# Strassen's scheme for the two branch projections of a hybrid decoder layer: seven products of token halves for eight, and the merged result through HBM

## Chip, cores and metric

One core of one Trainium2 chip. The metric is the device time of one execution in microseconds. TensorE is called PE here, VectorE DVE, ScalarE ACT, GpSimd POOL, and SP is the engine that issues most transfers.

## The reference

One layer for a prompt of 1024 tokens and 8 single sample tokens, model width 1024, all in float32. From the normed input one wide projection gives the inputs of two branches (retention, sliding-window attention) and two merge gates. What the change touches is the end of the layer:

```
br_r = jnp.einsum('bte,ed->btd', o_r, w_br_ret)
...
br_s = jnp.einsum('bte,ed->btd', o_s, w_br_swa)
merged = jax.nn.sigmoid(mg_r) * br_r + jax.nn.sigmoid(mg_s) * br_s
y = x + jnp.einsum('btd,de->bte', merged, w_out)
```

`o_r` and `o_s` are the branch outputs (tokens x 1024), `w_br_ret`, `w_br_swa` and `w_out` are 1024 x 1024.

## The kernel before

All matrices are held with the feature on the 128 partitions: 1024 features are 8 blocks (`KT`), the 1032 token columns (`TOK`, prompt and sample together) lie along the free axis. For precision each float32 operand is split into a hi and a lo part of type float32r, and each product is made of three matmuls: hi x hi, hi x lo, lo x hi (`gemm_T`, lines 212 to 214). Weights arrive by `load_unit`: a transfer of 512 KB into `wraw` (three buffers, `RAW`), a hi copy on ACT (line 168), a lo copy on POOL (line 169), with six slots for the pairs (`wbufs`). `run_steps` walks a list of steps and loads weight units a few steps ahead while slots are free.

The order of the work inside an engine is not the order of the program: a planner (the tile framework's scheduler, driven by its own timeline) takes for each engine the earliest instruction in program order that is ready and has a buffer, and the queues then run in that fixed order. A tile pool has a number of buffers per tag, and pools stacked on the left or the right side of SBUF reuse each other's place, tile by tile, when the older pool is closed.

Phase 1 makes the branch outputs. Per group of heads a gated output block is written to HBM (`d_o[0..7]` for retention, `d_o[8..15]` for attention, line 290), and 48 merge-gate blocks (`mg_block`, lines 292 to 299) write tanh values to `d_t`. The last of these merge-gate blocks end phase 1 on PE. Under them `open_a` (line 829) already loads seven of the eight retention operands back through the `oT` tiles (two buffers) and splits them with `split_op` (ACT line 870, DVE line 871) into the pool `opA1`.

`phase23` (line 879) then runs
- retention's projection: for each of 8 output blocks `c` and 3 token thirds `nb` (`BL` = 344 columns) 24 matmuls into one PSUM bank, then `br_r` multiplies with the gate (`tt`, loaded from `d_t`) and writes `d_m`. The eighth operand `opA7` and all eight attention operands `opB0..7` are loaded and split meanwhile, through `st` (two buffers);
- attention's projection in the same loops; `br_s` gates, adds the retention part (`mm`, loaded from `d_m`) and splits the merged block into `mhi` and `mlo`, which stay in SBUF;
- the output projection: two halves of 512 columns, each 8 token tiles and one of sample rows (`out_tile`, lines 943 to 959), with the merged blocks as stationary operand.

All loads and stores of these stages but the `d_t` writes stand in SP's queue.

Of the kernel before, what the change touches and what calls it, by code (L numbers as in the profile page):

```python
# [9 lines left out]
F32 = mybir.dt.float32  # L10
F32R = mybir.dt.float32r
AF = mybir.ActivationFunctionType
ALU = mybir.AluOpType
# [4 lines left out]
P = 128  # L18
# [92 lines left out]
def br_unit(w, c):  # L111
    return ("T", ((w, c * P, P),), 0, KT)


def out_unit(half, j):
    return ("o", (("w_out", half * 512, 512),), 2 * j, 2)
# [6 lines left out]
class Body:  # L123
# [27 lines left out]
    def load_unit(self, spec):  # L151
        nc = self.nc
        kind, segs, k0, nk = spec
# [16 lines left out]
        return view(hi), view(lo)  # L170

# [34 lines left out]
    def gemm_T(self, ps, unit, op, n0):  # L206
        nc = self.nc
        whi, wlo = unit
        cs = slice(n0, n0 + BL)
        for k in range(KT):  # L210
            hi, lo = op[k]
            nc.tensor.matmul(ps, whi[:, k, :], hi[:, cs], start=(k == 0), stop=False)  # L212
            nc.tensor.matmul(ps, whi[:, k, :], lo[:, cs], start=False, stop=False)  # L213
            nc.tensor.matmul(ps, wlo[:, k, :], hi[:, cs], start=False, stop=(k == KT - 1))  # L214

# [432 lines left out]
    def build(self):  # L648
# [4 lines left out]
        with tc.tile_pool(name="const", bufs=1, reuse_waits="tile") as cp, tc.tile_pool(name="sm", bufs=2, reuse_waits="tile") as sm, \  # L653
# [8 lines left out]
            self.d_m = [self.t(dp, [P, TOK], f"d_m{k}") for k in range(8)]  # L662
# [24 lines left out]
    def groups(self):  # L687
# [141 lines left out]
        def open_a(us):  # L829
            use(None)  # L830
            self.pA1 = self.tc.tile_pool(name="opA1", bufs=1, side="right", reuse_waits="tile")
            pool = self.pA1.__enter__()
            self.opA = []
            for k in range(0, NA1, 2):
                st = self.t(self.gp, [P, 2, TOK], "oT", bufs=2)
                for i in range(min(2, NA1 - k)):
                    nc.sync.dma_start(out=st[:, i, :], in_=self.d_o[k + i])
                    self.opA.append(self.split_op(pool, f"opA{k + i}", st[:, i, :], k + i))
        steps.append(([], open_a))
        steps += prev + mg  # L840
        steps.append(([br_unit("w_br_ret", 0), br_unit("w_br_ret", 1)], nop))
# [23 lines left out]
    def split_op(self, pool, tag, src, kt):  # L865
        nc = self.nc
        hi = self.t(pool, [P, TOK], tag + "h", F32R)
        lo = self.t(pool, [P, TOK], tag + "l", F32R)
        sc = self.scales[kt]
        nc.scalar.activation(out=hi[:], in_=src, func=AF.Copy, scale=sc)  # L870
        nc.vector.scalar_tensor_tensor(out=lo[:], in0=src, scalar=sc, in1=hi[:].bitcast(F32), op0=ALU.mult, op1=ALU.subtract)
        return hi, lo

    def load_op(self, pool, tag, kt):
        st = self.t(self.stg, [P, TOK], "st", bufs=2)
        self.nc.sync.dma_start(out=st[:], in_=self.d_o[kt])
        return self.split_op(pool, tag, st[:], kt)

    def phase23(self):
        nc, tc = self.nc, self.tc  # L880
        with tc.tile_pool(name="stg", bufs=1, reuse_waits="tile") as self.stg, tc.tile_pool(name="pacc2", bufs=8, space=PSUM, reuse_waits="tile") as self.pacc:
            pBc = tc.tile_pool(name="opB", bufs=1, reuse_waits="tile")
            pB = pBc.__enter__()
            with tc.tile_pool(name="opA2", bufs=1, side="right", reuse_waits="tile") as pA2:
                opA = self.opA + [self.load_op(pA2, f"opA{k}", k) for k in range(NA1, KT)]
                opB = [self.load_op(pB, f"opB{k}", 8 + k) for k in range(KT)]
                steps = []
                for c in range(KT):
                    for nb in range(NB):
                        steps.append(([br_unit("w_br_ret", c)], lambda us, c=c, nb=nb: self.br_r(us[0], c, nb, opA)))  # L890
                steps.append(([br_unit("w_br_swa", 0), br_unit("w_br_swa", 1)], nop))
                self.run_steps(steps, 2)
            self.pA1.__exit__(None, None, None)
            with tc.tile_pool(name="mrg", bufs=1, side="right", reuse_waits="tile") as pM:
                self.mhi = self.t(pM, [P, KT, TOK], "mhi", F32R)
                self.mlo = self.t(pM, [P, KT, TOK], "mlo", F32R)
                self.ms = self.t(self.stg, [P, KT, MROW], "st", F32R, bufs=2)
                nc.vector.memset(self.ms[:].bitcast(F32), 0.0)
                steps = []
                for c in range(KT):  # L900
                    for nb in range(NB):
                        steps.append(([br_unit("w_br_swa", c)], lambda us, c=c, nb=nb: self.br_s(us[0], c, nb, opB)))
                steps.append((([out_unit(0, j) for j in range(4)]), nop))
                self.run_steps(steps, 2)
                pBc.__exit__(None, None, None)
                steps = []
                with tc.tile_pool(name="fin", bufs=1, reuse_waits="tile") as self.fin:
                    for half in range(2):
                        us = [out_unit(half, j) for j in range(4)]
                        order = list(range(NT + 1)) if half == 0 else [NT] + list(range(NT))  # L910
                        for t in order:
                            steps.append((us, lambda u, half=half, t=t: self.out_tile(u, half, t)))
                    self.run_steps(steps, 4)

    def br_r(self, unit, c, nb, op):
        nc = self.nc
        n0 = nb * BL
        ps = self.t(self.pacc, [P, 512], "acc2")
        self.gemm_T(ps[:, :BL], unit, op, n0)
        tt = self.t(self.stg, [P, BL], "tt", bufs=2)  # L920
        nc.sync.dma_start(out=tt[:], in_=self.d_t[c][:, n0 : n0 + BL])
        nc.vector.scalar_tensor_tensor(out=tt[:], in0=tt[:], scalar=1.0, in1=ps[:, :BL], op0=ALU.add, op1=ALU.mult)
        nc.sync.dma_start(out=self.d_m[c][:, n0 : n0 + BL], in_=tt[:])

    def br_s(self, unit, c, nb, op):
        nc = self.nc
        n0 = nb * BL
        cs = slice(n0, n0 + BL)
        ps = self.t(self.pacc, [P, 512], "acc2")
        self.gemm_T(ps[:, :BL], unit, op, n0)  # L930
        tt = self.t(self.stg, [P, BL], "tt", bufs=2)
        mm = self.t(self.stg, [P, BL], "mm", bufs=2)
        nc.sync.dma_start(out=tt[:], in_=self.d_t[8 + c][:, cs])
        nc.sync.dma_start(out=mm[:], in_=self.d_m[c][:, cs])
        nc.vector.scalar_tensor_tensor(out=tt[:], in0=tt[:], scalar=1.0, in1=ps[:, :BL], op0=ALU.add, op1=ALU.mult)
        nc.vector.tensor_tensor(out=tt[:], in0=tt[:], in1=mm[:], op=ALU.add)
        nc.scalar.activation(out=self.mhi[:, c, cs], in_=tt[:], func=AF.Copy, scale=0.5)
# [49 lines left out]
```

## Time and profile before

| | |
|---|---|
| median of 3 runs (lowest, highest) | 1212.75 us (1212.04, 1216.18) |
| profiled execution, time | 1212.75 us |
| profiled execution, span of its instructions | 1211.0 us |
| mean granted clock of PE | 0.994 |
| PE busy | 1181.9 us (98%) |
| PE weight loads busy | 1115.3 us (92%) |
| DVE, ACT, POOL busy | 668.4, 457.1, 354.8 us |
| first matmul of a branch operand | 928.98 us |

The span is read as four parts: phase 1 up to 929 us, retention's projection up to about 1020, attention's up to about 1111, and the output projection to the end. Busy time of PE counts a matmul from start to modelled end, and matmuls overlap; what one costs in a full stream is the distance between two starts.

### The profile page before, as it was taken

Reading aid. Unit: us, or ns where it says so; the run is one execution under the profiler, and the core shown is the slowest. Engines: PE = TensorE matmul, PEld = TensorE weight load, DVE = VectorE, ACT = ScalarE, POOL = GpSimd, SP = SyncE. Lnnn points to the kernel's source line nnn. Section 1 sums busy time; section 2 is a strip of 40 time slices with the busy share of each in tenths; the row PEclk is TensorE's granted clock in tenths of the full one; section 3 lists DMA queues with packets and bytes.
Section 4 is the critical chain, followed back from the end, with each engine's and each line's share of the span. In section 5 each row is a group of like instructions: output and inputs, shape, how many; then the busy total and the mean of one; then the engine's idle time right before and its main releaser. Section 6 shows DMA issues by size and latency. Waiting matters only on the chain.

```text
span 1211.0 us, 19495 instructions
## 1 busy us (share of the span) xinstructions
PE 1181.9 (98%) x7228; PEld 1115.3 (92%) x7228; DVE 668.4 (55%) x2018; ACT 457.1 (38%) x1158; POOL 354.8 (29%) x282
## 2 busy tenths in 40 slices
PE   5799999999999999999999999999999999999998
PEld 4799999999989999999999999999899999999877
DVE  5455445544544387777776767677853411555121
ACT  5444334344334235554454445444544310221010
POOL 4424216315315433422242224112532122212010
PEclk9899999999999999999999999999999999999999
DMA  8414113223123411210141013101517844554221
GB/s 302 139 48 136 59 42 103 73 68 92 49 66 86 144 51 56 87 53 7 61 128 36 7 48 117 61 7 36 171 48 244 240 146 138 172 158 137 80 88 70
DMA packets 125169, 116.71 MB, mean 96 GB/s; under 512 B 17481, under 2 KB 113225, under 8 KB 125041
## 3 DMA queue, kind: packets, MB, share of 16 engines
q1 hardware_dynamic: 118160, 106.99, 28.5%
q10 hardware_dynamic: 6912, 8.46, 2.0%
q8 instruction: 57, 0.93, 0.3%
q14 instruction: 40, 0.32, 0.1%
HBM read 85.05 MB, written 32.44 MB: 97 GB/s over the span
## 4 chain that ended last, share of the span: by engine, by line
PE 92%; DVE 3%; DMA 1%; ACT 1%; issue 1%; SPq 1%; POOL 0%; ACTq 0%; POOLq 0%
PE acc L212 16%; PE acc L213 16%; PE acc L214 16%; PE acc L224 9%; PE acc L223 9%; PE acc L222 9%; PE tr L546 2%; PE acc L233 1%; PE acc L232 1%; PE av L441 1%; DMA oT<-in_x_prompt 1%; PE sc L532 1%; PE sc L533 1%; PE av L557 1%; DVE s L491 1%; PE av L556 1%
## 5 line engine op out<-in xcount | busy, mean ns | idle before, releaser
L169 POOL TENSOR_TENSOR wlo<-wraw,whi 128x1024 fp32r<-128x1024 f32 (+1 forms) x92 | 205.2, 2237 | 342.6 <-ACT whi L168 277.5
L212 PE MATMUL acc<-hhi,whi 128*128 128x344 f32 x864 | 281.9, 326 | 6.5 <-ACT whi L168 5.9
L213 PE MATMUL acc<-hlo,whi 128*128 128x344 f32 x864 | 279.8, 324 | 0.0
L214 PE MATMUL acc<-hhi,wlo 128*128 128x344 f32 x864 | 278.9, 323 | 0.0
L222 PE MATMUL acc<-whi,hhi 128*128 128x384 f32 x512 | 175.4, 343 | 2.4 <-ACT hhi L139 1.2
L223 PE MATMUL acc<-wlo,hhi 128*128 128x384 f32 x512 | 175.2, 342 | 0.6 <-POOL wlo L169 0.6
L224 PE MATMUL acc<-whi,hlo 128*128 128x384 f32 x512 | 175.3, 342 | 0.0
L212 PEld LDWEIGHTS acc<-hhi,whi 128*128 128x128 f32 x864 | 163.3, 189 | 8.6 <-ACT whi L168 6.2
L213 PEld LDWEIGHTS acc<-hlo,whi 128*128 128x128 f32 x864 | 163.2, 189 | 1.8 <-issue 1.0
L214 PEld LDWEIGHTS acc<-hhi,wlo 128*128 128x128 f32 x864 | 163.1, 189 | 1.4 <-issue 0.6
L147 POOL TENSOR_TENSOR rs<-ms,nhalf 128x1 f32<-128x1 f32 (+3 forms) x81 | 68.4, 846 | 295.1 <-DVE ms L146 286.4
L168 ACT ACTIVATE whi<-wraw 128x1024 fp32r<-128x1024 f32 (+1 forms) x92 | 90.2, 982 | 169.3 <-PE acc L213 106.3
L222 PEld LDWEIGHTS acc<-whi,hhi 128*128 128x128 f32 x512 | 97.5, 191 | 4.0 <-ACT hhi L139 1.6
L223 PEld LDWEIGHTS acc<-wlo,hhi 128*128 128x128 f32 x512 | 97.3, 190 | 2.5 <-POOL wlo L169 1.0
L224 PEld LDWEIGHTS acc<-whi,hlo 128*128 128x128 f32 x512 | 97.2, 190 | 0.5 <-DVE hlo L140 0.2
L486 ACT ACTIVATE s<-s,ng 128x256 f32<-128x256 f32 (+1 forms) x128 | 61.7, 485 | 25.8 <-DVE ng L483 25.7
L288 POOL TENSOR_TENSOR oT<-oT,tg 128x344 f32<-128x344 f32 x48 | 45.7, 954 | 84.9 <-DVE tg L286 62.2
L536 DVE CUSTOM_DVE_ANT_0 s<-sc,band,rs 128x256 f32<-128x256 f32 (+1 forms) x128 | 53.6, 460 | 19.4 <-PE sc L533 19.2
L139 ACT ACTIVATE pThi<-tr 128x512 fp32r<-128x512 f32 x60 | 35.3, 596 | 53.5 <-PE tr L546 53.1
L140 DVE TENSOR_TENSOR pTlo<-tr,pThi 128x512 fp32r<-128x512 f32 x60 | 41.0, 686 | 21.9 <-ACT pThi L139 21.7
L491 DVE TENSOR_SCALAR s<-s,r 128x256 f32<-128x256 f32 (+1 forms) x128 | 52.1, 468 | 0.7
L224 PE MATMUL acc<-whi,mlo 128*128 128x512 f32 x128 | 50.5, 395 | 0.0
(346 smaller groups left out, 2359.5 us busy)
## 6 DMA issues: line engine op xcount, KB each, us to landing
wraw<-in_w_in SPq DMA_DIRECT2D x36, 512.0 KB
d_t<-tg ACTq DMA_DIRECT2D x48, 172.0 KB
d_o<-oT SPq DMA_DIRECT2D x16, 516.0 KB
tt<-d_t SPq DMA_DIRECT2D x48, 172.0 KB
wraw<-in_w_in SPq DMA_DIRECT2D x32, 256.0 KB
st<-d_o SPq DMA_DIRECT2D x9, 516.0 KB
d_m<-tt SPq DMA_DIRECT2D x24, 172.0 KB
mm<-d_m SPq DMA_DIRECT2D x24, 172.0 KB
```

The source lines that it names most:

```text
L147: nc.gpsimd.tensor_tensor(out=rs[:p, :width], in0=ms[:p, :width], in1=self.nhalf[:p, :width], op=ALU.pow)
L168: nc.scalar.activation(out=hi[:, :f], in_=raw[:, :f], func=AF.Copy)
L169: nc.gpsimd.tensor_tensor(out=lo[:, :f], in0=raw[:, :f], in1=hi[:, :f].bitcast(F32), op=ALU.subtract)
L212: nc.tensor.matmul(ps, whi[:, k, :], hi[:, cs], start=(k == 0), stop=False)
L213: nc.tensor.matmul(ps, whi[:, k, :], lo[:, cs], start=False, stop=False)
L214: nc.tensor.matmul(ps, wlo[:, k, :], hi[:, cs], start=False, stop=(k == KT - 1))
L222: nc.tensor.matmul(ps, hi[:, k, a:b], whi[:, kk, :], start=(k == 0), stop=False)
L223: nc.tensor.matmul(ps, hi[:, k, a:b], wlo[:, kk, :], start=False, stop=False)
L224: nc.tensor.matmul(ps, lo[:, k, a:b], whi[:, kk, :], start=False, stop=(k == KT - 1))
L486: nc.scalar.activation(out=s[:p, j, :nk], in_=s[:p, j, :nk], func=AF.Exp, bias=ng[:p, j : j + 1], accum_out=l[:p, j : j + 1])
L491: nc.vector.tensor_scalar(out=s[:p, j, :nk], in0=s[:p, j, :nk], scalar1=r[:p, j : j + 1], scalar2=None, op0=ALU.mult)
L536: nc.vector.tensor_tensor_reduce(out=s[:, j, :nk], in0=sc[:, a, :nk], in1=band, scale=rs[:, j : j + 1], scalar=-3e38, op0=ALU.add, op1=ALU ...
```

## The change

Both branch projections use one level of Strassen's scheme in the form with seven products and shared sums. The two "rows" are two neighbouring output blocks `c` and `c + 1`, the two "columns" of the second operand are the two halves of the tokens, and the inner dimension is cut in two halves of four k-blocks (`j` and `j + 4`). The tokens are also cut in two quarters-of-halves `q` (`QTOK`: 256 columns each for q = 0, 260 for q = 1, which takes the sample tokens too), so that one product has 256 or 260 columns.

- Weights: per pair four parts (`load_part`): block 1, two sums, the changed block 2, one more sum, made by four DVE operations on `wsum` (one buffer) and split like before; 3.5 copies of 1024 columns per pair where there were two.
- Operands: `make_op` loads for one `j` four blocks of a quarter into `raw` (for retention it scales them on ACT), forms four differences on POOL, and splits seven matrices at once, hi on ACT and lo on DVE. A set is four such builds. The set for retention's q = 0 is made in `open_a` through the two `oT` buffers; the other three sets go through `raw` in pool `stg`, which has one buffer. Retention's two sets lie in `opA0` (right) and `opA1` (left); attention's sets take the same places when retention's last pair has used them (`swap`), and the merged blocks take them after that.
- `pair_steps`: seven products of 12 matmuls each, on four PSUM tiles, with three copies out of PSUM on ACT (`keep`) and four sums on DVE (`put`); then the gate as before.
- The merged block is written to HBM (`d_y`) by `br_s` and loaded and split again by `load_merged`, in two quarters; the output tiles of the first half run in the order 0, 1, 4, 5, 2, 3, 6, 7, sample rows.

```diff
+    def load_part(self, w, c, part):
...
+        one, two = self.praw
+        if part == 1:
+            sums = self.sums = self.t(self.sp, [P, 3, 512], "wsum", bufs=1)
+            a11, a12, a21, a22 = one[:, 0:512], one[:, 512:1024], two[:, 0:512], two[:, 512:1024]
+            nc.vector.tensor_tensor(out=sums[:, 1], in0=a21, in1=a22, op=ALU.add)
+            nc.vector.tensor_tensor(out=sums[:, 0], in0=sums[:, 1], in1=a11, op=ALU.subtract)
+            nc.vector.tensor_tensor(out=sums[:, 2], in0=a12, in1=sums[:, 0], op=ALU.subtract)
+            nc.vector.tensor_tensor(out=a21, in0=a11, in1=a21, op=ALU.subtract)
...
+        nc.scalar.activation(out=hi[:, :f], in_=src, func=AF.Copy)
+        nc.gpsimd.tensor_tensor(out=lo[:, :f], in0=src, in1=hi[:, :f].bitcast(F32), op=ALU.subtract)
...
+    def product(self, ps, part, half, op, b, start=True, stop=True):
...
+        for j in range(4):
+            ws = slice(half * 512 + j * P, half * 512 + (j + 1) * P)
+            hi, lo = op[j]
...
+            nc.tensor.matmul(ps[:, :n], whi[:, ws], hi[:, b, :], start=(start and j == 0), stop=False, **kw)
+            nc.tensor.matmul(ps[:, :n], whi[:, ws], lo[:, b, :], start=False, stop=False, **kw)
+            nc.tensor.matmul(ps[:, :n], wlo[:, ws], hi[:, b, :], start=False, stop=(stop and j == 3), **kw)
...
+        def keep():
+            sn = self.t(self.stg, [P, 260], "sn", bufs=3)
+            nc.scalar.activation(out=sn[:, :n], in_=v["X"][:, :n], func=AF.Copy)
+            return sn[:, :n]
...
+        a, m, b, d = units
+        return [([a], p1), ([a], p2), ([m], p6), ([m], p5), ([b], p7), ([b], p4), ([d], p3)]
...
+            raw = lambda: self.t(self.gp, [P, 2, TOK], "oT", bufs=2)[:].rearrange("p a b -> p (a b)")
+            self.opA0 = [self.make_op(pool, raw(), 0, j, 0) for j in range(4)]
...
+    def make_op(self, pool, raw, base, j, q):
+        nc = self.nc
+        n = QTOK[q]
+        r = raw[:, : 8 * n].rearrange("p (a n) -> p a n", a=8)
+        for e in range(2):
+            k = j + 4 * e
+            self.get_quarter(r[:, 2 * e : 2 * e + 2], self.d_o[base + k], q)
+            if base == 0:
+                nc.scalar.activation(out=r[:, 2 * e : 2 * e + 2], in_=r[:, 2 * e : 2 * e + 2], func=AF.Copy, scale=self.scales[k])
+        b12, b11, b22, b21, t1, t2, t3, t4 = [r[:, a] for a in range(8)]
+        for o, a, b in ((t1, b12, b11), (t2, b22, t1), (t3, b22, b12), (t4, t2, b21)):
+            nc.gpsimd.tensor_tensor(out=o, in0=a, in1=b, op=ALU.subtract)
+        hi = self.t(pool, [P, 7, n], f"op{j}h", F32R)
+        lo = self.t(pool, [P, 7, n], f"op{j}l", F32R)
+        nc.scalar.activation(out=hi[:], in_=r[:, 1:], func=AF.Copy)
+        nc.vector.tensor_tensor(out=lo[:], in0=r[:, 1:], in1=hi[:].bitcast(F32), op=ALU.subtract)
...
+        raw = lambda: self.t(self.stg, [P, 8 * 260], "raw", bufs=1)[:]
...
+            ops(("r", 1), 0, 1)(self.pL.__enter__())
+            steps = []
+            for b, w, fin in (("r", "w_br_ret", self.br_r), ("s", "w_br_swa", self.br_s)):
+                for c in range(0, KT, 2):
+                    for q in range(2):
+                        steps += self.pair_steps(w, c, q, (lambda b=b, q=q: op[b, q]), fin)
+                        if c == KT - 2:
+                            attr, side = ("pR", right) if q == 0 else ("pL", left)
+                            if b == "r":
+                                steps.append(swap(attr, lambda side=side, q=q: side(f"opB{q}"), ops(("s", q), 8, q)))
+                            else:
+                                steps.append(swap(attr, lambda side=side, q=q: side(f"m{q}"), merged(q)))
...
+    def load_merged(self, k, q):
...
+        st = self.t(self.stg, [P, 2, 260], "st", bufs=2)
+        hi, lo = self.mq[q]
+        nc.sync.dma_start(out=st[:, :, :n], in_=self.d_y[k, q][:])
+        nc.scalar.activation(out=hi[:, k], in_=st[:, :, :n], func=AF.Copy, scale=0.5)
+        nc.vector.scalar_tensor_tensor(out=lo[:, k], in0=st[:, :, :n], scalar=0.5, in1=hi[:, k].bitcast(F32), op0=ALU.mult, op1=ALU.subtract)
```

## Rows read from the trace of the kernel before

**Rows 1.** The page: busy time by engine, and the last chain by engine.

```profile
PE 1181.9 (98%) x7228; PEld 1115.3 (92%) x7228; DVE 668.4 (55%) x2018; ACT 457.1 (38%) x1158; POOL 354.8 (29%) x282
PE 92%; DVE 3%; DMA 1%; ACT 1%; issue 1%; SPq 1%; POOL 0%; ACTq 0%; POOLq 0%
```

**Rows 2.** Stretches: from:to, length, busy time (instructions) by engine, clock, DMA share, GB/s.

```profile
929.00:1032.00 103.00, 103.00 (x654) 102.81 (x654) 25.98 (x35) 20.30 (x20) 21.72 (x9) 1.00 0.57 174
1032.00:1111.00 79.00, 79.00 (x502) 79.00 (x501) 46.32 (x83) 18.48 (x31) 16.79 (x7) 1.00 0.54 167
1111.00:1211.00 100.00, 96.25 (x416) 75.36 (x415) 18.50 (x25) 4.67 (x6) 7.17 (x3) 1.00 0.23 79
```

**Rows 3.** Timeline of PE: start us, us, instruction; eight of 256 columns, then the next.

```profile
442.76 0.28 PE L532 MATMUL sc<-kThi,qs 128*128 128x256 f32 x1
...
443.71 0.34 PE L224 MATMUL acc<-whi,hlo 128*128 128x384 f32 x1
```

**Rows 4.** Timelines of SP, ACT, DVE: two loads and their first users, [idle before <-releaser].

```profile
946.89 0.32 SPq L876 DMA_DIRECT2D st<-d_o  x1
951.89 1.07 ACT L870 ACTIVATE opB3h<-st 128x1032 fp32r<-128x1032 f32 x1 [3.39 <-DMA st<-d_o]
...
1005.02 0.32 SPq L921 DMA_DIRECT2D tt<-d_t  x1
1007.34 0.51 DVE L922 SCALAR_TENSOR_TENSOR tt<-tt,acc 128x344 f32<-128x344 f32 x1 [4.82 <-DMA tt<-d_t]
```

**Rows 5.** POOL by line and shape: xcount | busy us, mean ns | idle before <-releasers.

```profile
L169 POOL TENSOR_TENSOR wlo<-wraw,whi 128x1024 fp32r<-128x1024 f32 x60 | 144.2, 2407 | 302.7 <-ACT whi L168 246.3 <-PE acc L233 42.8 <-ACT vv L139 5.5
...
L641 POOL TENSOR_TENSOR Aswa_q_g<-s,gbs 128x288 f32<-128x288 f32 x1 | 0.8, 793 | 0.0
```

**Rows 6.** ACT by line and shape.

```profile
L168 ACT ACTIVATE whi<-wraw 128x1024 fp32r<-128x1024 f32 x60 | 63.3, 1057 | 154.4 <-PE acc L213 100.0 <-PE acc L232 43.6 <-DMA wraw<-in_w_in 6.5
...
L139 ACT ACTIVATE pThi<-tr 128x512 fp32r<-128x512 f32 x60 | 35.3, 596 | 53.5 <-PE tr L546 53.1
L168 ACT ACTIVATE whi<-wraw 128x768 fp32r<-128x768 f32 x32 | 26.9, 842 | 14.8 <-PE acc L213 6.3 <-DMA wraw<-in_w_in 4.7 <-PE acc L224 2.0
```

**Rows 7.** Timeline of DVE: lo copies of 1032 columns, the first while POOL works.

```profile
913.25 1.91 DVE L871 SCALAR_TENSOR_TENSOR opA0l<-oT,rng,opA0h 128x1032 fp32r<-128x1032 f32 x1 [0.20 <-ACT opA0h L870]
...
922.19 1.29 DVE L871 SCALAR_TENSOR_TENSOR opA2l<-oT,rng,opA2h 128x1032 fp32r<-128x1032 f32 x1 [5.16 <-ACT opA2h L870]
...
941.45 1.23 DVE L871 SCALAR_TENSOR_TENSOR opB0l<-st,opB0h 128x1032 fp32r<-128x1032 f32 x1 [0.44 <-ACT opB0h L870]
```

**Rows 8.** Timelines of SP and DVE: the first loads of mm and their first use.

```profile
948.81 0.42 SPq L934 DMA_DIRECT2D mm<-d_m  x1
...
1033.78 0.52 DVE L936 TENSOR_TENSOR tt<-tt,mm 128x344 f32<-128x344 f32 x1
```

**Rows 9.** Timeline of PE where the branch projections begin.

```profile
928.98 0.32 PE L212 MATMUL acc<-opA0h,whi 128*128 128x344 f32 x1
...
931.81 0.32 PE L212 MATMUL acc<-opA0h,whi 128*128 128x344 f32 x1
...
939.74 0.75 PE L212 MATMUL acc<-opA7h,whi 128*128 128x344 f32 x3
```

**Rows 10.** Timelines of ACT and SP while open_a loads operands.

```profile
912.07 1.14 ACT L870 ACTIVATE opA0h<-oT,rng 128x1032 fp32r<-128x1032 f32 x1
...
917.06 2.59 SPq L837 DMA_DIRECT2D oT<-d_o  x4
```

**Rows 11.** Stretches around two slow stretches of the clock (columns as in rows 2).

```profile
31.30:38.10 6.80, 4.55 (x14) 4.56 (x15) 1.67 (x4) 3.67 (x6) 4.23 (x3) 0.50 1.04 330
...
857.00:860.70 3.70, 1.90 (x13) 1.48 (x11) 3.70 (x3) 0.46 (x1) 3.40 (x2) 1.00 0.91 245
860.70:864.10 3.40, 3.40 (x13) 3.24 (x14) 3.32 (x14) 1.87 (x4) 0.20 (x1) 0.51 1.03 335
864.10:868.00 3.90, 3.90 (x28) 3.84 (x27) 3.36 (x6) 2.08 (x4) 3.34 (x2) 0.99 0.76 224
```

More of the change, by code (lines that the diff above doesn't have):

```diff
@@ L108, in shape_constants, with pair_units @@
     return {k: np.ascontiguousarray(v.astype(np.float32)) for k, v in out.items()}
-def br_unit(w, c):
-    return ("T", ((w, c * P, P),), 0, KT)
+def pair_units(w, c):
+    return [("S", w, c, part) for part in range(4)]
+HALF = SEQ // 2
+QTOK = (256, 260)
+B11, B22, B21, T1, T2, T3, T4 = range(7)
 def out_unit(half, j):
@@ L152, in load_unit @@
         nc = self.nc
+        if spec[0] == "S":
+            return self.load_part(*spec[1:])
         kind, segs, k0, nk = spec
@@ L830, in open_a @@
             use(None)
[L831 to L838, printed above, removed]
+            self.pS = self.tc.tile_pool(name="wsum", bufs=1, side="right", reuse_waits="tile")
+            self.sp = self.pS.__enter__()
+            self.pR = self.tc.tile_pool(name="opA0", bufs=1, side="right", reuse_waits="tile")
+            pool = self.pR.__enter__()
+            raw = lambda: self.t(self.gp, [P, 2, TOK], "oT", bufs=2)[:].rearrange("p a b -> p (a b)")
+            self.opA0 = [self.make_op(pool, raw(), 0, j, 0) for j in range(4)]
         steps.append(([], open_a))
         steps += prev + mg
-        steps.append(([br_unit("w_br_ret", 0), br_unit("w_br_ret", 1)], nop))
+        steps.append((pair_units("w_br_ret", 0)[:2], nop))
         self.run_steps(steps, 2)
@@ L863, in swa_consts, with quarter, get_quarter @@
             nc.sync.dma_start(out=dst[:], in_=self.i[name][0].rearrange("b k g d -> k b (g d)"))
-    def split_op(self, pool, tag, src, kt):
+    def quarter(self, t, q):
+        return t[:, :SEQ].rearrange("p (h q n) -> p q h n", h=2, q=2)[:, q], t[:, SEQ:].rearrange("p (h n) -> p h n", h=2)
+    def get_quarter(self, dst, src, q):
         nc = self.nc
[L867 to L871, printed above, removed]
+        body, rows = self.quarter(src, q)
+        nc.sync.dma_start(out=dst[:, :, :256], in_=body)
+        if q:
+            nc.sync.dma_start(out=dst[:, :, 256:260], in_=rows)
@@ L872, in split_op @@
         return hi, lo
[L874 to L877, printed above, removed]
     def phase23(self):
         nc, tc = self.nc, self.tc
-        with tc.tile_pool(name="stg", bufs=1, reuse_waits="tile") as self.stg, tc.tile_pool(name="pacc2", bufs=8, space=PSUM, reuse_waits="tile") as self.pacc:
[L882 to L913, printed above, removed]
@@ new lines, in phase23, with swap, fn @@
+        op = {("r", 0): self.opA0}
+        raw = lambda: self.t(self.stg, [P, 8 * 260], "raw", bufs=1)[:]
+        left = lambda name: tc.tile_pool(name=name, bufs=1, reuse_waits="tile")
+        right = lambda name: tc.tile_pool(name=name, bufs=1, side="right", reuse_waits="tile")
+        def swap(attr, mk, fill):
+            def fn(us):
+                getattr(self, attr).__exit__(None, None, None)
+                ctx = mk()
+                setattr(self, attr, ctx)
+                fill(ctx.__enter__())
+            return ([], fn)
@@ new lines, in ops, with fill, merged @@
+        def ops(key, base, q):
+            def fill(pool):
+                op[key] = [self.make_op(pool, raw(), base, j, q) for j in range(4)]
+            return fill
+        def merged(q):
+            def fill(pool):
+                self.mq[q] = tuple(self.t(pool, [P, KT, 2, QTOK[q]], f"m{q}{x}", F32R) for x in "hl")
+                if q:
+                    nc.vector.memset(self.ms[:].bitcast(F32), 0.0)
+                for k in range(KT):
+                    self.load_merged(k, q)
+            return fill
@@ new lines, in phase23 @@
+        with tc.tile_pool(name="stg", bufs=1, reuse_waits="tile") as self.stg, tc.tile_pool(name="pacc2", bufs=8, space=PSUM, reuse_waits="tile") as self.pacc:
+            self.ms = self.t(self.stg, [P, KT, MROW], "ms", F32R)
+            self.mq = {}
+            self.pL = left("opA1")
+            ops(("r", 1), 0, 1)(self.pL.__enter__())
[10 more added lines that the diff above has]
+                                steps.append(swap(attr, lambda side=side, q=q: side(f"m{q}"), merged(q)))
+            for half in range(2):
+                us = [out_unit(half, j) for j in range(4)]
+                order = [0, 1, 4, 5, 2, 3, 6, 7, NT] if half == 0 else [NT] + list(range(NT))
+                for t in order:
+                    steps.append((us, lambda u, half=half, t=t: self.out_tile(u, half, t)))
+            self.run_steps(steps, 4)
+            self.pL.__exit__(None, None, None)
+            self.pR.__exit__(None, None, None)
+            self.pS.__exit__(None, None, None)
```

109 lines of the change are left out of this document (81 added, 28 removed).

## The prediction

> **What bounds the kernel now.** First the engines' table and the chain that ended last [rows 1]: TensorE (PE) is busy for 98% of the span and carries 92% of the chain, so work taken from PE is worth its full price, and anything that makes PE wait costs its full price too. Then the stages the change touches [rows 2]: from 929 to 1032 us PE runs one matmul every 103.0/654 = 157.5 ns and has no idle time, the same from 1032 to 1111; the output projection fills the last 100 us. The branch projections are 2 branches x 8 output blocks x 3 token thirds x 24 = 1152 matmuls of 344 columns, 1152 x 157.5 ns = 181.4 us. Nobody else is near a limit there: from 929 to 1032 VectorE is busy 26 us, ScalarE 20, GpSimd 22 of 103. So the question is only whether PE gets shorter work and stays fed.
>
> **Matmuls: a gain of 20.6 us.** Per pair of output blocks and token quarter there are 7 products x 4 k-pairs x 3 = 84 matmuls; 4 pairs x 2 quarters x 2 branches give 1344, half of 256 columns and half of 260. Eight matmuls of 256 columns back to back start from 442.76 to 443.71, 0.95/8 = 118.8 ns each, every one with its own weight load [rows 3]. Against 157.5 at 344 that is 0.44 ns a column, so 260 columns take 120.5. The mean is 119.6: 1344 x 0.1196 = 160.8 us, 20.6 less. One quarter of one pair (84) is 10.0 us. The bounds: if long trains keep the old pitch of 157.5 the term is +30 us; I see no reason for under 118.
>
> **One operand build: 10.7 to 12.3 us, one after another.** The new operands (7 matrices, hi and lo) are built per k-pair `j`, four builds to a set, in four sets: (ret, q0), (ret, q1), (swa, q0), (swa, q1). Each build is a row of dependent steps: load into `raw`, (ret only) two scalings, four subtractions, one hi copy, one lo copy. Outside the first set `raw` is a tag with one buffer, so the next load waits until the lo copy has read it: nothing overlaps inside a set.
> - Load: two transfers of 256 KB (q1: two small ones more). A load of 172 KB was used 2.3 us after its issue (1005.02 to 1007.34), one of 516 KB 5.0 us after (946.89 to 951.89) [rows 4]. The bytes are those of the second, but that one shared a busy queue; I take the middle, 3.65, and 4.45 for q1, whose two further issues take SP some 0.4 each (0.32 for the instruction [rows 4]). Bounds 2.3 and 5.0.
> - Subtractions on GpSimd, 256 elements: 0.79 us at 288 and 2.41 at 1024 [rows 5], so 2.2 ns an element and 0.72 each, 2.9 for four.
> - Hi copy on ScalarE, 1792 elements: 1.057 at 1024 and 0.842 at 768 [rows 6] give 1.70. The scalings are 0.6 each (0.59 at 512); the first lies beside the second load, so 0.8 counts.
> - Lo copy on VectorE, 1792 elements: 1.23 to 1.29 at 1032 [rows 7], against 0.51 at 344 [rows 4], so 2.05 alone; a first bound of 1.9 and, beside GpSimd, 1.91/1.29 as long, 3.0.
> - Hand-overs: some 0.1 each, 0.4.
>
> Sum: 10.7 (swa, q0), 11.5 (swa, q1), 12.3 (ret, q1); with the bounds together 9.3 to 14.
> The lo copy beside GpSimd took 1.91, without it 1.29 [rows 7]. The Trainium skill, "SBUF — State Buffer", section "Who interferes with whom", says that a VectorE instruction with two SBUF inputs and a GpSimd one that reads SBUF exclude each other for the whole instruction; the trace agrees, and by the rule a lo copy that meets a weight copy would stand up to 2.4 us late, up to 9.6 us a set, where my sum has nothing: four sets late by that would give 1332 instead of 1294.
>
> **What covers a set.** Operands are overwritten in place: a swa set may write its hi and lo only when the ret operands of that quarter have been read for the last time. The planner orders by readiness, not by program order, and fills PE with what it can: before, while the eighth operand was late, PE started three blocks with the seven it had (block two starts at 931.81, before the first is ended, three opA7h in one go at 939.74) [rows 9]. It also loads ahead into a free buffer: `mm` issued at 948.81 is used at 1033.78 [rows 8]. So I grant: (a) the first `raw` of a set is loaded and subtracted ahead where it is free; (b) products of the waiting quarter run for the k-pairs that are there, 4 accumulators x 9 = 36 matmuls, 4.3 us; (c) while a q1 set is awaited, the next pair's q0 runs, but only its first two weight parts fit (six slots, four held by the current pair), 48 matmuls, 5.7 us. More the weight slots do not allow.
> - (swa, q0): its operands are free when ret's last q0 ends. First build 1.70 + 2.05 = 3.8, three more 32.1: 35.9. Cover: ret's last q1, 10.0, and 4.3. **Stall 21.6** (bounds 17 to 30).
> - (swa, q1): `raw` is free only when (swa, q0) is done: 4 x 11.5 = 46. Cover: the other 48 matmuls of q0, 5.7, plus 5.7, plus 4.3 = 15.7. **Stall 30.3** (22 to 38).
> - (ret, q1): `raw` now lies where the two `oT` tiles were, which hold the loads of (ret, q0); so it too starts when that set ends. 4 x 12.3 = 49.2 - 15.7: **stall 33.5** (25 to 46, with weight copies of 2.41 in the same GpSimd queue).
> - (ret, q0): two buffers here, under the merge-gate blocks that end at 928.98 [rows 9]. The first build takes the place of opA0h at 912.07; the loads that need released `oT` come at 917.06 and later [rows 10]. From 917 two builds in a row on one buffer, 11.5 each, end at 940, 11 after PE is free, less 4.3: **stall 7** (3 to 12).
>
> **The rest.** Merged blocks now go to HBM and back (`load_merged`, 8 a quarter, two buffers): 3.3 us for two (load 2.3 and ACT and DVE copies of 512), some 15 us for eight against 10.0 of the last swa q1 and output tiles that start on k-blocks present: 2 (0 to 8). The second quarter's reload lies beside four output tiles of 24 x 0.231 us (96.25/416 in the last stage [rows 2]), 22 us in all, at nothing; without that cover 15. SP's queue holds all loads in planner order; the weight loads for the pairs stand between them and are early by a pair. The sums of weight blocks (four of 512 on VectorE) and 28 instead of 16 weight copies' worth on GpSimd (28 x 2.41 = 67 us of 160) lie beside PE at nothing once it streams. Evictions (`keep`, `put`: under the 0.51 of 344 columns [rows 4]) have one product, 1.4 us, of cover each.
>
> **The clock.** When PE had been idle for half of 857.0 to 860.7, the granted clock stood at 0.51 for the next 3.4 us, 13 matmuls where the next stretch has 28 in 3.9; earlier it stood at 0.50 for 6.8 us [rows 11]: each return costs 1.7 to 3.4 us. Four long stalls: 8 (6.8 to 13.6). The Trainium skill, "TensorE: Matmul & The Clock Gate", Part 1, says that the slow clock is the default and activity lifts it; the trace agrees, and the rule speaks against a change that cuts PE's stream; without it the sum would come to 1286.
>
> **The sum**: -20.6 + 7 + 33.5 + 21.6 + 30.3 + 2 + 8 = +81.8 us. The profiled execution took 1212.75 with a span of 1211.0; it is the median of the runs shown, so nothing is to be added: 1212.75 + 81.8, **1294 us**. With all low ends 1266, with all high ends about 1339.
>
> **Rivals.**
> - *Builds overlap* (the other side). If the steps of a set ran side by side, a build every 2.9 us (GpSimd, the longest), a set would take 3.8 + 8.7 = 12.5, under 14.3 of cover; stalls go to 3, the clock's part to 2, and the time is 1212.75 - 20.6 + 3 + 2 + 2 = 1199. It decides at a set under about 14 us. For it: in the first set, on two buffers, it partly holds. Against it: one `raw` buffer. 0.07.
> - *The planner covers more*: half of the three large stalls go because `raw` finds free memory or more products move ahead: 1294 - 43 = 1251. For it: [rows 9]. Against: six weight slots. 0.13.
> - *The trains do not hold 119 ns*: PE's weight loads are 188 ns long and fill the 344-column stage (102.81 of 103 us [rows 2]). If loads set the pace in long trains, pitch 157.5: 1294 + 51 = 1345. Against: rows 3 have a load each. 0.05.
> - *Queues in planner order run wrong on the chip*: VectorE or ScalarE holds a copy of a build behind an eviction that waits for PE; one eviction's product train (10 us) in each of three sets: 1324. 0.08.
> - That the products are not fewer is excluded by the count, 1344 shorter matmuls.
>
> **How the numbers follow.** Forecast 0.67, rivals as given. The range reaches from the second rival's upper half to the forecast's high end: 1243 to 1338. Faster by over 0.3% (about what a measurement of this kernel can tell from no change) has the first rival and little else, 0.08; within 0.3% 0.02; slower 0.90.
>
> **What would show it.** In the profile after: PE idle four times, for some 7, 33, 22 and 30 us, each ended by the hi or lo tile of the fourth build (`op3h`, `op3l`); `raw` loads one by one, 10 us or more apart; matmuls of 256 columns 119 ns apart in between; the granted clock at half after each stall. Wrong it is if PE stays over 95% busy between 929 us and the end, if raw loads of one set overlap, or if the pitch at 256 columns is over 125 ns.

## The result, and the profile after

| | before | after |
|---|---|---|
| median (lowest, highest) | 1213.45 us (1212.04, 1216.18) | 1318.14 us (1317.50, 1322.59) |
| profiled execution, span | 1211.0 us | 1315.7 us |
| mean granted clock of PE | 0.994 | 0.953 |

The change made the kernel slower: ratio 1.0865, 95% interval 1.0841 to 1.0889, 104.7 us between the medians. The forecast was 1294 us, in a range of 1243 to 1338.

The page of the kernel after, engines and granted clock in 40 slices (before: [rows 1]):

```profile
PE 1194.8 (91%) x7420; PEld 1117.1 (85%) x7420; DVE 748.2 (57%) x2082; ACT 505.0 (38%) x1230; POOL 438.2 (33%) x362
...
PEclk9899999999999999999999999999868967699999
```

PE's share fell from 98% to 91%, and the granted clock dips in the slices of the branch projections. The busy time of PE even rose, from 1181.9 to 1194.8, although its matmuls in the changed stages are cheaper: a matmul at half clock counts for longer. The chain that ended last is of no use here: its shares add up to about a tenth of the span.

The stages of the kernel after, cut at the first matmul of a branch product, at the first use of the fourth operand (`op3l`) of each of the four operand sets, and where retention's last q = 0 product and the stream before the output projection end (columns as in [rows 2], which has the same stages of before):

```profile
core 0: us, PE busy (x) PEld busy (x) DVE busy (x) ACT busy (x) POOL busy (x), PEclk, DMA share, GB/s
927.94:945.27 17.33, 7.61 (x41) 6.71 (x41) 7.51 (x4) 7.61 (x7) 9.97 (x10) 0.82 0.29 89
945.27:991.44 46.17, 22.80 (x120) 20.69 (x120) 11.44 (x11) 13.63 (x15) 11.96 (x16) 0.65 0.43 115
991.44:1057.35 65.91, 62.10 (x488) 60.87 (x489) 35.88 (x46) 19.38 (x35) 31.70 (x18) 0.96 0.49 143
1057.35:1095.11 37.76, 13.99 (x67) 12.11 (x65) 16.69 (x16) 8.76 (x7) 14.32 (x15) 0.60 0.38 114
1095.11:1140.19 45.08, 21.49 (x120) 19.39 (x120) 12.91 (x12) 7.92 (x7) 11.74 (x16) 0.65 0.35 95
1140.19:1207.42 67.23, 62.68 (x501) 61.50 (x501) 43.49 (x53) 20.42 (x36) 32.66 (x14) 0.97 0.57 176
1207.42:1315.70 108.28, 100.99 (x430) 77.60 (x428) 35.50 (x64) 14.61 (x21) 10.12 (x5) 0.98 0.42 136
```

Rows 1, 2, 4 and 5 of the seven are the waits for the four sets, each with few matmuls in a long time; rows 3 and 6 are the streams behind them. Who ended PE's waits, from the first branch product to the output projection (us in total, times, longest):

```profile
PE acc L257 <- ACT op3h L989: 22.0, 4, 7.1
PE acc L257 <- ACT op2h L989: 20.6, 3, 7.8
PE acc L257 <- ACT op1h L989: 15.4, 4, 4.7
PE acc L257 <- ACT sn L273: 7.4, 9, 1.4
PE acc L258 <- DVE op0l L990: 6.1, 1, 6.1
...
PE acc L257 <- DVE cc L280: 3.1, 4, 1.7
```

78 of some 89 us of waiting are for the hi and lo tiles of operand builds. One build, the last of retention's q = 1 set, in the timelines of SP, ACT, POOL and DVE (start, length, what):

```profile
980.13 0.36 SPq L971 DMA_DIRECT2D raw<-d_o  x1
...
991.42 0.87 SPq L971 DMA_DIRECT2D raw<-d_o  x2
...
983.05 0.73 ACT L983 ACTIVATE raw<-raw,rng 128x520 f32<-128x520 f32 x1 [5.04 <-DMA raw<-d_o]
...
987.58 1.72 ACT L989 ACTIVATE op3h<-raw 128x1820 fp32r<-128x1820 f32 x1 [2.27 <-POOL raw L986]
...
985.44 2.11 POOL L986 TENSOR_TENSOR raw<-raw 128x260 f32<-128x260 f32 x3 [0.85 <-ACT raw L983]
...
989.33 2.06 DVE L990 TENSOR_TENSOR op3l<-raw,op3h 128x1820 fp32r<-128x1820 f32 x1 [9.23 <-ACT op3h L989]
```

Load from 980.13, first scaling at 983.05, subtractions to 987.55, hi copy to 989.30, lo copy to 991.39, and only at 991.42 the next load, since `raw` has one buffer: 11.3 us, step behind step, where 12.3 were forecast for this set.

### The profile page after: what moved, and what is told of

It reads as the page before. It is cut to its first block, busy times and chain, and to the rows that moved or that the text cites. A ratio compares the mean times of both kernels' runs of the same rounds, so it can differ in the third digit from the quotient of the medians.

```text
span 1315.7 us, 20230 instructions
## 1 busy us (share of the span) xinstructions
PE 1194.8 (91%) x7420; PEld 1117.1 (85%) x7420; DVE 748.2 (57%) x2082; ACT 505.0 (38%) x1230; POOL 438.2 (33%) x362
## 5 line engine op out<-in xcount | busy, mean ns | idle before, releaser
L176 POOL TENSOR_TENSOR wlo<-wraw,whi 128x1024 fp32r<-128x1024 f32 (+1 forms) x76 | 167.4, 2212 | 187.3 <-ACT whi L175 125.2
L175 ACT ACTIVATE whi<-wraw 128x1024 fp32r<-128x1024 f32 (+1 forms) x76 | 73.3, 967 | 80.4 <-PE acc L246 41.9
L986 POOL TENSOR_TENSOR raw<-raw 128x260 f32<-128x260 f32 (+1 forms) x48 | 35.4, 758 | 91.7 <-DMA raw<-d_o 57.1
L257 PE MATMUL acc<-op3h,whi 128*128 128x260 f32 (+1 forms) x112 | 32.4, 311 | 22.0 <-ACT op3h L989 22.0
```

Source lines behind the costliest of these rows:

```text
L175: nc.scalar.activation(out=hi[:, :f], in_=raw[:, :f], func=AF.Copy)
L176: nc.gpsimd.tensor_tensor(out=lo[:, :f], in0=raw[:, :f], in1=hi[:, :f].bitcast(F32), op=ALU.subtract)
```

## Experiments

Each is an edit of the kernel after. Medians, with the ratio to the kernel before:

| | us | ratio (95%) |
|---|---|---|
| attention uses retention's sets | 1256.75 | 1.0350 (1.0332 to 1.0369) |
| eleven builds reduced to their copies | 1242.32 | 1.0243 (1.0222 to 1.0263) |
| both | 1230.52 | 1.0123 (1.0106 to 1.0140) |
| two `raw`, small buffers cut | 1296.21 | 1.0673 (1.0657 to 1.0688) |
| two `raw`, output rows cut | 1277.22 | 1.0516 (1.0500 to 1.0533) |
| that, and subtractions on DVE | 1264.54 | 1.0417 (1.0396 to 1.0437) |
| subtractions on DVE | 1302.54 | 1.0729 (1.0705 to 1.0753) |
| extra matmuls in the waits | 1322.24 | 1.0894 (1.0854 to 1.0934) |
| merged load without the store | 1322.22 | 1.0880 (1.0859 to 1.0901) |

**Are the sets the cost?** First, without attention's two sets:

```diff
-  steps += self.pair_steps(w, c, q, (lambda b=b, q=q: op[b, q]), fin)
+  steps += self.pair_steps(w, c, q, (lambda b=b, q=q: op["r", q]), fin)
...
-  if b == "r":
-      steps.append(swap(attr, ..., ops(("s", q), 8, q)))
```

> Attention's products run on retention's two operand sets, so the two attention sets are never loaded and built; that part of the computation (the attention operands) is left out, all matmuls, weights, gates and the merged blocks stay. Theory (the serial builds of sets are where the time goes): the changed kernel lost 30.1 us up to the first use of the last operand of attention's q = 0 set and 30.7 us up to that of its q = 1 set; without the builds most of it goes, about 1318 - 61 = 1257 us, range 1250 to 1268. Rival (the matmul stream itself, its weight parts or the order of the queues are slow, and the waits only stand where the stream would be slow anyway): less than a third of it goes, 1295 us or more.

1256.75: 61.4 us less, where the two waits lost 60.8. All 1182 branch matmuls from retention's second set on now run as one stretch:

```profile
993.23:1151.32 158.09, 151.14 (x1206) 147.43 (x1207) 100.09 (x130) 44.78 (x79) 69.55 (x31) 0.99 0.58 175
```

The granted clock is 0.99 and POOL, DVE and the weight parts keep up. So a slow stream is not the cause. Then the builds' loads, scalings and subtractions alone:

```diff
+  if (base, q) != (0, 0) and (base, j) != (0, 0):
+      r = self.kept[:, :, :n]
+      hi = self.t(pool, [P, 7, n], f"op{j}h", F32R)
+      lo = self.t(pool, [P, 7, n], f"op{j}l", F32R)
+      nc.scalar.activation(out=hi[:], in_=r[:, 1:], func=AF.Copy)
+      nc.vector.tensor_tensor(out=lo[:], in0=r[:, 1:], in1=hi[:].bitcast(F32), op=ALU.subtract)
+      return hi, lo
...
```

> Only retention's q = 0 set and the first operand of its q = 1 set are built in full; every other operand is split (hi on ACT, lo on DVE) from the one loaded and subtracted block, which is kept: no loads, scalings and subtractions for 11 of 16 builds, so those operands are left out of the computation. Theory (serial builds): the 31.9, 30.1 and 30.7 us lost in the three sets shrink to what two copies per operand leave, first operand 3.8 us and then one in 2.1 us, about 4 us of wait a set: 1318 - 93 + 12 = 1237 us, range 1227 to 1250. What is above 1213 - 21 = 1192 is then the cost of the rest (first set, trains, merged blocks, clock). Rival (slow stream or queues): 1290 us or more. Rival (the copies, not the loads and subtractions, set the pace of a build): 1270 us or more.

1242.32, inside the theory's range: the copies alone don't set the pace of a build; its loads, scalings and subtractions hold most of it. Both edits at once:

> The two edits of the first two runs together: attention's products run on retention's sets, and retention's q = 1 set but for its first operand is split from one kept block. One full set, one cheap one; the rest of the operands is left out of the computation. Theory (losses by set add up): 1257 for the run without attention's sets, less the 31.9 us of retention's q = 1 set, plus about 5 that its copies leave: 1230 us, range 1222 to 1237. Then even three sets of four at next to no cost leave the scheme slower than the kernel before, since the 20.6 us that 1344 matmuls at 119.6 ns save are less than the first set, the trains and the end lose. Rival (the sets hide each other's cost, and with all gone the saving shows): 1213 us or less.

1230.52, as added up. So the cost per set is separable, and with three of four sets gone or nearly so the kernel is still 1.2% slower than the one before. What PE waits for in that run, besides the sets:

```profile
PE acc L257 <- ACT sn L273: 6.1, 9, 1.9
PE acc L323 <- ACT m0h L1082: 4.9, 2, 4.6
```

**Is it the one buffer?** A second buffer for `raw` takes 8320 bytes a partition, which other tiles have to give; two ways of paying for them.

```diff
-  raw = lambda: self.t(self.stg, [P, 8 * 260], "raw", bufs=1)[:]
+  raw = lambda: self.t(self.stg, [P, 8 * 260], "raw", bufs=2)[:]
```

The first way leaves `tt` and `mm` one buffer each and `x`, the output rows, two of four. The second leaves `tt` and `mm` alone and lets the output rows use the two buffers of `mm`:

```diff
-  x = self.t(self.stg, [P, 512], "x", bufs=4)
+  x = self.t(self.stg, [P, 2, 260], "mm", bufs=2)[:].rearrange("p a b -> p (a b)")[:, :512]
```

The first way:

> The whole computation, with two raw buffers where there was one, paid for with one buffer less for the gate tile and the retention part and two less for the output rows. Theory (a build is a serial chain of load, subtractions and copies, and the chains of two operands stand one behind the other only because of the one buffer): the pace of builds falls from 9.7 to 11.4 us to half of it, 5 to 6, as no engine works more than about 5 us on one; three sets gain three paces each, 3 x 3 x 5 = 45 us at most: 1273 us, range 1262 to 1290. Rival (an engine or the DMA queue is the limit of a build, POOL with DVE shut out beside it, say): 1300 us or more.

1296.21, outside the theory's range and inside neither rival. The waits did shrink as the theory has it (31.8 to 16.2 us and 30.7 to 11.2 for the two q = 1 sets), but attention's stream lost 22.6 us up to the output projection, where it had lost 7.4. Its waits, 1099 to 1200 us:

```profile
PE acc L257 <- DVE cc L280: 10.7, 6, 3.4
```

The sums `cc` had become late: either for want of the gate and retention buffers taken away, or because denser builds crowd DVE. (The 35.7 and 17.5 us in the text below run on to the last branch matmul, and so hold 36 and 24 matmuls of the output projection.) The second way tells the two apart:

> The whole computation; two raw buffers as in the run before, but the place comes from the output rows alone, which share the two buffers of the retention part; the gate tile and the retention part keep two buffers. In the run before, the losses before the last operand of a set fell from 31.8 to 16.2 us (retention, q = 1) and from 30.7 to 11.2 us (attention, q = 1), but attention's stream behind them lost 35.7 us where it had lost 17.5, with 10.7 us of waits for the sums of DVE. Theory (those waits came from the buffers taken away): 1296 - 16 = 1280 us, range 1273 to 1287. Rival (they come from the denser builds themselves, through DVE, POOL or SP's queue): 1292 us or more.

1277.22, the first of the two: the late sums came from the buffers of the gate and the retention part; which of the two tiles wasn't taken apart. The sets' stages in it, retention q = 1 and attention q = 1, and ACT's hi copies in the former, after those of the same set with one buffer (its fourth, at 987.58, stands above):

```profile
946.31:976.96 30.65, 20.08 (x121) 18.71 (x121) 11.93 (x11) 13.52 (x15) 18.64 (x19) 0.72 0.56 156
...
1072.91:1098.13 25.22, 18.56 (x120) 17.43 (x120) 14.31 (x12) 7.93 (x7) 16.12 (x15) 0.84 0.47 122
```

```profile
952.98 1.72 ACT L989 ACTIVATE op0h<-raw 128x1820 fp32r<-128x1820 f32 x1 [2.03 <-POOL raw L986]
964.73 1.72 ACT L989 ACTIVATE op1h<-raw 128x1820 fp32r<-128x1820 f32 x1 [2.82 <-POOL raw L986]
976.30 1.72 ACT L989 ACTIVATE op2h<-raw 128x1820 fp32r<-128x1820 f32 x1 [2.27 <-POOL raw L986]
```

```profile
953.63 1.72 ACT L989 ACTIVATE op0h<-raw 128x1820 fp32r<-128x1820 f32 x1
958.25 1.73 ACT L989 ACTIVATE op1h<-raw 128x1820 fp32r<-128x1820 f32 x1 [2.18 <-POOL raw L986]
966.97 1.70 ACT L989 ACTIVATE op2h<-raw 128x1820 fp32r<-128x1820 f32 x1
972.79 1.72 ACT L989 ACTIVATE op3h<-raw 128x1820 fp32r<-128x1820 f32 x1 [3.49 <-POOL raw L986]
```

The same 120 matmuls take 30.65 us for 46.17, and 25.22 for 45.08. With one buffer the hi copies are 11.5 us apart on average. With two they come in pairs, 4.6 and 5.8 us apart, and a pair follows the other after 13.3 us: two chains side by side, as many as there are buffers, each somewhat slower than one alone, 6.4 us a build. This settles the main step of the forecast: the one buffer made the builds serial.

**Which steps are in the chain?** Subtractions on DVE, alone and with the two buffers:

```diff
-  nc.gpsimd.tensor_tensor(out=o, in0=a, in1=b, op=ALU.subtract)
+  nc.vector.tensor_tensor(out=o, in0=a, in1=b, op=ALU.subtract)
```

> The whole computation; the four subtractions of a build run on DVE, not on POOL. Theory (a build is a serial chain, in which POOL's part is 2.84 us): a lo copy of 1032 columns took DVE 1.29 us, 1.24 ns a column, so 4 x 260 x 1.24 = 1.3 us here, 1.5 us less a build. Twelve to sixteen builds lie on the path: 18 to 24 us less, 1297 us, range 1290 to 1306. Rival (the loads or DVE's copies set the pace of the builds): 1314 to 1322 us.

1302.54, 15.6 less and in range. The chain lost less than expected, for a subtraction took DVE 0.425 us where 0.32 had been estimated (duration ns, least/median/most):

```profile
L986 DVE TENSOR_TENSOR raw<-raw x48: 410/425/2244, 949.2 to 1121.9; 128x260 f32<-128x260 f32 x32, 128x256 f32<-128x256 f32 x16
```

4 x (0.73 - 0.425) = 1.2 us a build, 14.6 for twelve builds. The trace of this run bears it out: the stages that hold the three later sets (the second with retention's stream) are 3.1, 5.2 and 5.9 us shorter, 14.2 in all. The first set gave nothing: its wait is 4.4 us shorter, but the branch products begin 4.6 us later.

Then both, on the second way of having two buffers:

> The whole computation; the two raw buffers of the kernel ahead of this one and DVE for the four subtractions, both. Theory (a buffer's cycle of load, subtractions and copies still sets the pace, two builds at a time): each pair of builds gets 1.5 us shorter, 2 pairs x 3 sets x 1.5 = 9 us, and the first set up to 3 us: 1280 - 10 = 1270 us, range 1260 to 1277. Rival (with two buffers DVE, with its copies and now the subtractions, or the DMA queue sets the pace): no more than 3 us better than with two buffers alone.

1264.54, 12.7 less than with two buffers alone. So shorter steps still help with two builds at a time, and DVE with the four subtractions added doesn't set their pace. It is the fastest version that computes everything with the scheme, and still 50 us behind the kernel before.

**What does the half clock cost?** Some 114 us lie at the lower level (1.2 of 2.4 GHz): twice the missing share of the clock, times the length, added over the rows of the stages above. In this run one PSUM bank goes from the accumulators to the extra matmuls, and the output rows have three buffers of four.

```diff
+  one = self.t(self.stg, [P, 256], "one", F32R)
+  nc.vector.memset(one[:].bitcast(F32), 1.0)
...
   self.run_steps(steps, 4)
+  wps = self.t(pw, [P, 512], "warm")
+  for i in range(268):
+      nc.tensor.matmul(wps[:, :256], one[:, :P], one[:], start=True, stop=True)
```

> The whole computation, with 268 extra matmuls of 256 columns on a constant into a PSUM bank of their own, which the planner sets where PE waits (one PSUM buffer and one for the output rows less). They take the waits, not the work: 211 of the 1344 branch matmuls began in stretches of half granted clock at 215 ns apart, against 120. Theory A (half clock costs what the forecast gave it, 8 us, as most of these matmuls run inside the waits): 1318 - 8 + about 4 for extra matmuls that stand ahead of work = 1314 us, range 1308 to 1320. Theory B (all 211 lie on the path): 211 x 0.095 = 20 us less, 1298 to 1303. Rival (the clock doesn't follow the gaps in PE's work): the half-clock stretches stay and the time is 1318 us or above.

1322.24 (1317.21 to 1329.59), no gain. The profiled execution is the slowest of the four. The planner put 231 of the extra matmuls into the wait for retention's q = 1 set:

```profile
949.26:996.34 47.08, 44.59 (x351) 43.77 (x352) 11.79 (x12) 13.78 (x15) 11.90 (x16) 0.96 0.38 108
```

There the granted clock rose from 0.65 to 0.96, and the stage took 47.08 us for 46.17. So the granted clock follows the gaps in PE's work, against the rival, and half clock inside this wait cost nothing, against theory B: the 120 matmuls of the stage fit into the waits at either level. The time is 4 us above instead of 4 below, a difference within the spread of this run's executions. In the profiled one, the branch products begin 4.0 us later than in the kernel after; retention's stream with attention's first wait is 4.8 us longer, as the other 37 extra matmuls stand ahead of its work (37 x 0.119 = 4.4); and the stretch from the output projection's start is 6.8 us longer, with 5.7 us of waits for `m0h`. Whether that comes from the PSUM bank or the buffer taken away was not tried. Nor did the extra matmuls reach attention's waits, so the finding is shown for one set of four.

**What does the way through HBM cost?** The merged load without its store:

```diff
-  nc.sync.dma_start(out=st[:, :, :n], in_=self.d_y[k, q][:])
+  nc.sync.dma_start(out=st[:, :, :n], in_=self.d_m[k, q][:])
```

> The merged blocks are loaded from the retention part that was stored long before, not from the merged part that was stored last: the load waits for no store, and the output leaves the attention part out. Theory (the way through HBM costs what the end lost, 6.9 us against 2 of the forecast): 3 to 6 us less, 1313 us, range 1310 to 1316. Rival (the end loses its time to the place and the split of the merged blocks, not to store and load): within 2 us of 1318.

1322.22, nothing gained; the theory falls, and the time lies 2 us above the rival's range too. PE still waits in the output projection for the split of merged blocks:

```profile
PE acc L323 <- ACT m0h L1074: 4.1, 2, 3.9
PE acc L325 <- DVE m0l L1075: 2.4, 1, 2.4
```

So the end doesn't lose its time to the wait for the store. What PE waits for first can be read from the trace of the kernel after, where it waits 2.4 us for `m0l` as well, and 1.0 for `m0h` (timelines of ACT, POOL and DVE):

```profile
1205.72 1.14 ACT L1074 ACTIVATE m0h<-st 128x512 fp32r<-128x512 f32 x2
...
1208.69 2.36 POOL L176 TENSOR_TENSOR wlo<-wraw,whi 128x1024 fp32r<-128x1024 f32 x1 [0.66 <-ACT whi L175]
...
1209.47 2.12 DVE L1053 SCALAR_TENSOR_TENSOR cc<-tt,cc 128x512 f32<-128x512 f32 x1
1211.52 1.28 DVE L1075 SCALAR_TENSOR_TENSOR m0l<-st,m0h 128x512 fp32r<-128x512 f32 x2
```

The hi copies of the first two blocks were done at 1206.86, so their place was free and their loads were there; the lo copies began only at 1211.52, behind other work in DVE's queue, at its end a gate that took 2.12 us beside a weight copy on POOL (0.69 alone). The wait for `m0h` is that of a later block, whose hi copy waited for its load: the way back from HBM, through the two buffers of `st`, keeps a part, and no run took that part away.

## Why the prediction was right, and where its terms were off

Losses of the kernel after: length of a stage less the branch matmuls that start in it (40, 120, 488, 64, 120, 500 and 12) x 0.1196 us; for the last stage, also less the 100 us that the output projection took before.

| term | forecast | measured |
|---|---|---|
| matmuls | -20.6 | -20.6 at the pitch assumed |
| wait for (ret, q0) | 7 | 12.5 |
| wait for (ret, q1) | 33.5 | 31.8 |
| wait for (swa, q0) | 21.6 | 30.1 |
| wait for (swa, q1) | 30.3 | 30.7 |
| clock | 8 | in the streams |
| streams of retention and attention | 0 | 7.5 + 7.4 |
| merged blocks and end | 2 | 6.9 |
| sum | +81.8 | +106.3 |

The branch products also began 1.0 us sooner than before, which leaves 105.3, against 104.7 between the spans. The mechanism stood as forecast: four waits, each ended by the last operand of a set, loads of `raw` one by one, and PE busy for 75% of the time from 929 us on (291.05 of 386.70), where over 95% would have refuted it. In size the forecast was 24 us low: 5.5 for (ret, q0), 8.5 for (swa, q0), 6.9 for the streams with the clock, 4.9 for the end, less 1.3 for the other two sets. These are the terms:

- **The pitch held.** The timeline of PE where retention's q = 0 ends:

```profile
1056.28 0.28 PE L259 MATMUL acc<-op0h,wlo 128*128 128x256 f32 x1
...
1057.34 0.28 PE L259 MATMUL acc<-op3h,wlo 128*128 128x256 f32 x1
...
1065.63 0.58 PE L258 MATMUL acc<-op0l,whi 128*128 128x256 f32 x1 [6.12 <-DVE op0l L990]
1066.01 0.42 PE L259 MATMUL acc<-op0h,wlo 128*128 128x256 f32 x1
...
1067.30 0.41 PE L259 MATMUL acc<-op0h,wlo 128*128 128x256 f32 x1
1067.51 0.42 PE L257 MATMUL acc<-op0h,whi 128*128 128x260 f32 x1
```

  Nine steps from 1056.28 to 1057.34: 118 ns, against 118.8 in [rows 3]. At half clock, six steps from 1066.01 to 1067.30: 215 ns.
- **Two sets out of four were sized to 2 us**, with builds about as long as worked out (11.5 us apart in both, for 12.3 and 11.5) and nearly the cover granted: 120 matmuls in each of the two q = 1 stages, for 48 + 48 + 36 = 132. A little luck is in it: at (ret, q1) a chain 3 us shorter than forecast, whose load was used 2.9 us after its issue where 4.45 had been taken, made up for 1.4 us less of cover.
- **(swa, q0) had half of its cover.** The forecast granted 84 matmuls of retention's last q1 and 36 partial ones, 14.3 us. In the trace, when the last q0 product had ended (1057.34), the planner had long mixed the two quarters, and 24 of the 84 were left; 12 of these stood in PE's queue behind eight matmuls that wait for `op0l`, and ran from 1067.51. 64 matmuls instead of 120 are 6.7 us less of cover, and the set took 37.8 us for 35.9: that is the 8.5 us. Why the planner mixed them wasn't tried; the step that failed is that a quarter's last product would come first because it stands first in the program.
- **`op0l` was late on DVE**, twice, which explains most of the 6.12 us above and of (ret, q0). Timelines of DVE and POOL in the two places:

```profile
913.51 2.91 DVE L195 TENSOR_TENSOR wsum<-wraw,wsum 128x512 f32<-128x512 f32 x1
916.35 4.23 DVE L990 TENSOR_TENSOR op0l<-oT,op0h 128x1792 fp32r<-128x1792 f32 x1
...
915.82 2.87 POOL L202 TENSOR_TENSOR wlo<-wraw,whi 128x1024 fp32r<-128x1024 f32 x1
...
1060.40 0.43 DVE L280 TENSOR_TENSOR cc<-acc,sn 128x260 f32<-128x260 f32 x1 [2.32 <-ACT sn L273]
1060.74 2.30 DVE L1053 SCALAR_TENSOR_TENSOR cc<-tt,cc 128x512 f32<-128x512 f32 x1
1062.96 0.68 DVE L193 TENSOR_TENSOR wsum<-wraw 128x512 f32<-128x512 f32 x1
1063.57 2.01 DVE L990 TENSOR_TENSOR op0l<-raw,op0h 128x1792 fp32r<-128x1792 f32 x1
...
1067.98 0.69 DVE L1053 SCALAR_TENSOR_TENSOR cc<-tt,cc 128x520 f32<-128x520 f32 x1
...
1060.15 2.34 POOL L202 TENSOR_TENSOR wlo<-wraw,whi 128x1024 fp32r<-128x1024 f32 x1 [2.01 <-ACT whi L201]
```

  At (ret, q0) `op0h` was done at 911.9. The four weight sums stood ahead of `op0l` on DVE until 916.4, the last taking 2.91 us for 0.68, and `op0l` itself took 4.23 instead of 2.01, both beside weight copies on POOL. So the next load of the set was issued at 920.60, not at 917.06 as in [rows 10]: 3.5 of the 5.5 us. The forecast had the weight sums on DVE at nothing. The Trainium skill, "SBUF — State Buffer", section "Who interferes with whom", says that a DVE instruction with two SBUF inputs and a GpSimd one that reads SBUF shut each other out; the trace agrees. The forecast had that as a price of up to 9.6 us a set and took nothing for it; in the three later sets, whose lo copies mostly took 2.05 us, it was next to nothing for the copies themselves.

  At (swa, q0) `op0h` was done at 1058.6 and `op0l` began 4.9 us later, mostly through the order of DVE's queue: DVE first waited until 1060.40 for an eviction (`sn`, which on ACT stood behind a weight copy), then came its sum, a gate that took 2.30 us for 0.69 beside a weight copy on POOL, and a weight sum. POOL's part in these 4.9 us is 1.6.
- **Evictions were not free.** The forecast gave `keep` and `put` one product of cover. PE waited 2.4 us for `sn` and 1.4 for `cc` in retention's stream, 2.8 and 1.7 in attention's: 8.3 us.
- **The clock was about right.** The two streams and the end have 5.3, 4.0 and 4.3 us of half clock (twice the missing share), in which half the work is done: at most 6.8 us lost, against 8. Its part in the two streams, 4.6, and the evictions' 8.3 make 12.9 of the 14.9 that they lost. The rest comes with the eleven waits for the evictions: a wait is counted from the end of the matmul before, 0.28 us after its start, where in the stream the next starts after 0.12, and 11 x 0.16 = 1.8.
- **The merged blocks** cost 6.9 for 2, within the bounds of 0 to 8, and not through the wait for the store; 2.4 us are the lo copies that stood behind the last gates on DVE.

Of the rivals, overlapping builds needed a second buffer: with one it didn't come, with two it came in part. What it would have been worth was optimistic: even with three sets out of the way the time was 1230.5, not 1199, since (ret, q0), the evictions and the end stay. The rival of queues in the wrong order showed in small: at (swa, q0), where DVE held `op0l` behind an eviction that wasn't ready and PE held 12 ready matmuls behind the 6.12 us of wait, and in the 2.4 us for `m0l`; nowhere was it 10 us a set. That the trains don't hold their pitch is excluded by the 118 ns; that the planner covers more, by the waits.

## What to carry to other kernels

A scheme that saves multiplications pays with operand preparation: compare the saving (here 20.6 us of 181) with the serial time of preparing one operand set, times the sets that must take the place of one still in use. As a first estimate, count a chain's pace as the sum of its steps divided by the buffers of the tile that all of them share (here 11.5 us a build with one buffer and 6.4 with two, a little over half), and look for the memory for that buffer where nothing on the path is prefetched. Cover that rests on the order in which a planner sets ready work was, in the one set where that order mattered, worth half of what the program's order promised.

## What the runs showed of the hardware

- Half clock inside a wait for data cost nothing in the one stage where it was tried: raising the granted clock from 0.65 to 0.96 there left its length as it was (46.17 and 47.08 us).
- Short bursts of PE, one as each operand came, did not keep the clock up: the granted clock was 0.60 to 0.65 in the mean of the three long waits, between its two levels of 1.2 GHz (0.50) and 2.4 GHz (1.00).
- A high busy share of weight loads was no bound: they fill the stream of 344 columns at 157.5 ns a matmul [rows 2], and yet 256 columns, with a weight load in front of every matmul too, ran at 118 ns, with the loads busy for 92% of the stage (60.87 of 65.91 us).
- DVE operations with both inputs in SBUF took longer beside a weight copy on POOL: a gate over 512 columns 2.30 us, and one over 520 columns 0.69 without it; a lo copy over 1792 columns 4.23 us, and 2.01.
